# Making one pair of output-projection weights in the other order, and shifting side steps in the attention heads of a hybrid decoder layer

## The chip, the cores and the metric

The kernel runs on one core of one Trainium2 chip. The metric is the device time of one execution, in microseconds. Three runs of the kernel before gave 2347.37, 2345.92 and 2347.12 us, a median of 2347.12 us. Engines are named as the profile names them: PE multiplies matrices, DVE is the vector engine, ACT the scalar engine, POOL the GpSimd engine, SP the engine that issues most of the DMA transfers.

## The reference

One layer with 1024 tokens and 2048 features in float32: normalise, project to the queries, keys, values and gates of two groups of eight heads, run stick-breaking attention on one group and differential attention on the other, gate, project out, add to the residual, then a second gated projection of an embedding and a final norm. Cut to what matters here:

```python
hn = rmsnorm(x, norm_mix_g)
sb_q, sb_k, sb_v, sb_g, df_q, df_k, df_v, df_g = split(hn @ w_in)
sb_out = stick_breaking_attention(sb_q, sb_k, sb_v)        # 8 heads of 128
df_out = differential_attention(rope(df_q), rope(df_k), df_v, lam)   # 8 heads, 2 x 64 query/key columns
mixed = concat([sb_out * silu(sb_g), rmsnorm(df_out) * silu(df_g)])
h = x + mixed @ w_out                                       # the output projection
h = h + sigmoid(rmsnorm(h) @ w_ple_gate) * (p @ w_ple_proj)
return rmsnorm(h) * norm_final_g
```

## The kernel before

Activations are held transposed, with 128 features on the partitions and the tokens in two halves of 512. A float32 product is three matmuls: each operand is split into a high part, rounded to the PE's fast float32 form, and a low part, the rest; high times high, high times low and low times high go into one PSUM bank. Splitting is one ACT instruction (the high part) and one DVE instruction (the low part).

The program runs in five stages, one after the other: the projection to values and gates; the heads of token half 1; the heads of token half 0; the output projection; the gate projection with the final norm. The values-and-gates projection and the output projection save multiplications with seven products in place of eight (Strassen's scheme in Winograd's form), over sums of quarter blocks; the class `Seven` holds what they share.

**The heads.** Each head is a unit of 32 triples of matmuls (lines 263 to 265) that make the head's queries and keys. After every triple the program calls `side.tick()`, which advances a counter and runs the side steps that have come due: the attention of the head before, the gates, the loading and splitting of later operands. A step's due time is a number in the tables at the head of the file, counted in triples. A due time therefore sets only the place of the step's instructions in the program. Each engine works through its own instructions in that order and stops at one whose operand is not there. PE, DVE and ACT keep the written order; for SP and POOL a scheduler in the build places the transfers.

Steps and lines that the prediction speaks of:

- `taken` of a stick-breaking head (line 1611) multiplies the finished query or key sums by the row factors on DVE; the high parts follow on ACT (line 1619), the low parts on DVE (line 1614), and then the scores can start (lines 341 to 343).
- In the differential heads of half 0 a score block z (lines 345 and 346) lies in a PSUM tile of which there are two. It is masked and reduced to a row maximum on DVE (line 326), then exponentiated on ACT (line 402), which lets the tile go. Each head has eight such blocks, two for each of four groups of query rows.
- `turn` and `mix` transpose the finished weights (line 484), split them (lines 501 to 507) and multiply by the values (lines 527 to 532). `norm` sums squares with a small matmul (line 573).
- At the seam, the last unit of half 1, `swap` loads the normalised input of half 0 over that of half 1, as `late_x0`: line 1352 issues the load, and some ticks later lines 1355 (ACT) and 1356 (DVE) split it.

**The output projection.** It has two phases of eight columns of blocks, u = 0 to 7. In the second phase PE runs, for each u, the products A11(u), A22(u-1), S2(u), S4(u-1), A12(u), S1(u), S3(u), each of twelve matmuls (lines 713 to 715). After each product `step` prepares weights for a later one: `whigh` casts the high part on ACT (line 804, or 802 for S4, which is negated), `wlow` subtracts for the low part on DVE (line 818, or 816 for S4). The weights are made in a fixed order, about four products ahead of their use, into a ring of nine tiles. The sources are four raw quarter blocks B11, B12, B21, B22 of the weight matrix and three differences made on DVE (line 769): T1 = B12 - B11 and T2 = B22 - T1 with S2, T3 = B12 - B22 with S3, T4 = B21 - T2 with A22. B21 is the source of A12, and T4 is the last reader of B21: right behind T4 the program issues the load of B21 for the next u (line 760). `u3` (line 1968, shown as u) adds the S3 sums to the A11 result on DVE; the next A22 product goes into the same PSUM bank and must wait for it. Lines 1848 to 1856 are the sums for the next stage's operands, which follow the stored rows by fixed steps.

The order in which the weights are made is the list that `flow` returns:

```python
def flow(n):
    return [(ph, u, nm) for ph in range(2) for u in range(n) for nm in (("A11", "A12") if ph else ()) + ("S2", "S1", "S3", "S4", "A22")]
```

Of the kernel before, what the change touches and what calls it, by code (L numbers as in the profile page):

```python
# [31 lines left out]
EPS = 1e-6  # L32
SUB_EPS = 1e-5

SC = ((6.5, 7, 9.0, 11.5, 15.5, 17.5, 20.0, 21.5), (10.5, 10.5, 15.5, 23.0))
TT = ((19, 31, 16.0), (21.5, 36.5, 20))
DGAP = (3, 7.0)
DF0 = (0.5, 1, 1.5, 3.5, 5.5)
DF1 = (1, 1.0, 3, 5, 6.5)
LV = ((3.0, 4.0), (1, 2))  # L40
LT = ((1, 1.5), (0.5, 2.0))
LM = ((0.5, 2.0, 4, 5), (1.5, 2.5, 4.5, 6.5))
LN = ((1, 6.0), (1, 4.5))
PRIO = 300
NORM_LAT = ((8.0, 8.5), (13, 11))
XLAT = 5
SBB = ((20, 20, 15, 15.5, 16, 16.5, 16.5, 16.0), (19.5, 8.5, 5.0, 3.5, 4.0, 5.5, 5.0, 3.0))
SBS = ((0.5, 3.5, 15.5, 23.5), (-2.5, 3, 7.0, 13.0))
SBT = ((15, 31, 13), (16.0, 30.0, 14.5))
SGAP = (3.5, 6.0)  # L50
SBL = ((1.5, 3, 6.0), (1, 2, 8.0))
SVG = ((18, 37.5, 40, 40, 46), (30.5, 37.5, 41.0, 43.5, 49.5))
CST = (16.5, 19.5)
ROPE = ((-0.4, 1.5, 3.0, 4.0, 2.2, 4.5, 6.0, 7.0), (-1.9, -1, 0, 1, 0.20000000000000018, 2, 3, 4))
ROPE_ = ((3.5, 4.0, 6.0, 10.0, 11.6, 12.5, 15.0), (6.5, 7, 9.5, 12.5, 12.6, 13.5, 14))
VGD = ((19.5, 37, 37.0, 39.5, 44.0), (22.5, 32.5, 35.5, 37.0, 45.0))
LAM0 = 0.8 - 0.6 * math.exp(0.0)
NEG = -1.0e30
EXTRA = 5, 9
PIECES = 30  # L60
LOWG = ORDER1[H - 1:H + 1]
LAST = ((2.5, 3.5), (2, 4.0))
X1T = 1, 2.5, 4, 5.5, 9, 10.5, 12, 13.5
VLAG = 3

# [6 lines left out]
def _body(ctx, nc, tc, ap):  # L72
# [174 lines left out]
    side = Side()  # L247
# [66 lines left out]
    def attention(at, pz, half, hd, q, qz, K, KL, VV, sg, vg, state):  # L314
# [45 lines left out]
        def weights(rb, c):  # L360
# [3 lines left out]
            if sb:  # L364
# [125 lines left out]
        def parts(pr, g, tp, wh, wl):  # L490
# [18 lines left out]

            side.later(1 if sb else LT[half][0], high)  # L510
            side.later(2 if sb else LT[half][1], low)

        def mix(pr, g):
# [33 lines left out]

            side.later(2 if sb else LM[half][1], summed)
            if sb:
# [15 lines left out]

            side.later(LM[half][2], squared)
            side.later(LM[half][3], low)

        def norm(pr):
# [25 lines left out]

            side.later(LAST[half][0], roots)
            side.later(LAST[half][1], step)

        n0 = nb // 2
        n1 = n0 - 1  # L600
        gap = SGAP[half]
        if sb and half == 1 and hd == ORDER1[-1]:
            b = SBB[1][hd]
            ss, t0, t1, tv = [[b], [b + 4], [b + 10], [b + 15]], b + 17, b + 30, b + 14
        elif sb:
            b = SBB[half][hd]
# [11 lines left out]
        for pr, t, n in ((0, t0, n0), (1, t1, n1)):  # L618
# [5 lines left out]
            if not sb:  # L624
                steps.append((t + gap * n + NORM_LAT[half][pr], partial(norm, pr)))
        return steps

    with tc.tile_pool(name="at", bufs=2) as at, ExitStack() as banks:
# [26 lines left out]
        def ftile():  # L655
            return ev.tile([P, HALF], F32, name="hc", tag="f", bufs=4)

        def flow(n):
            return [(ph, u, nm) for ph in range(2) for u in range(n) for nm in (("A11", "A12") if ph else ()) + ("S2", "S1", "S3", "S4", "A22")]

        class Seven:

# [580 lines left out]
        for ph in range(2):  # L1243
            for u in range(2 * H):
                last = ph == 1 and u == 2 * H - 1
# [115 lines left out]

        op = Seven(lambda u, ph, k: ap["w_out"][u, ph, k], 8, flow(8))
        tw_d = dram.tile([8, 2, P, 2, HALF], F32, name="tw_d", tag="tw_d")
        hcomb_d = dram.tile([4, 8, P, HALF], F32, name="hcomb_d", tag="hcomb_d")
        q_d = dram.tile([8, 2, P, HALF], F32, name="q_d", tag="q_d")
# [152 lines left out]
        for half in (1, 0):  # L1520
# [5 lines left out]
            for hd in (ORDER0, ORDER1)[half]:  # L1526
# [27 lines left out]
                if half == 1 and hd == ORDER1[-1]:  # L1554
                    def late_x0(kt, wait):
                        with tc.issue_after(lastw[0].ins):
                            side.add([(wait, load_x0(kt))])

                    def swap(pc):
                        for i, kt in enumerate((pc * 2, pc * 2 + 8, pc * 2 + 1, pc * 2 + 9)):  # L1560
                            if pc < 2:
                                side.add([(1 + 4 * i, load_x0(kt))])
                            else:
                                side.add([(1 + i, partial(late_x0, kt, 4 + 3 * i))])

                    side.add([(8 * pc + 7, partial(swap, pc)) for pc in range(4)])

# [35 lines left out]
                if sb:  # L1603
# [26 lines left out]
                    side.add([(28, partial(taken, 0)), (31, partial(taken, 1))])  # L1630
                    side.add([(t, fn) for t, fn in zip(SVG[half], (load_vg, partial(normed, 0), partial(normed, 1), gate, gated))])
                    if half == 0 and hd == ORDER0[-1]:
                        last_steps()
                    unit(X, acc=acc)
                    q, k, qz, KL = qk[0], qk[1], None, None
                else:
# [63 lines left out]
                    q, k, qz, KL = qk[0], qk[1], qk["qz"], qk["kl"]  # L1700
# [21 lines left out]
                if half == 1 and hd >= H or half == 0 and 1 < hd < 6:  # L1722
                    kt = KT[hd if half else hd - 2]
# [759 lines left out]
```

## Time and profile before

| what | value |
|---|---|
| median of three runs | 2347.12 us |
| the profiled execution's own time | 2344.73 us |
| its span, first to last instruction | 2342.9 us |
| PE busy | 2300.4 us (98%) |
| DVE busy | 1828.0 us (78%) |
| ACT busy | 1170.5 us (50%) |
| heads of half 1 | from 619.5 us to 1062.8 us |
| heads of half 0 | from 1062.8 us to about 1640 us |
| output projection, second phase | from 1800.8 us to about 1965 us |

The times of the last three rows are the starts of the matmuls concerned in the trace. The span is 1.8 us shorter than the time of the same execution, which holds what lies before the first and behind the last instruction. In a row of the timeline the first number is the start in microseconds from the start of the span, the second the duration, then come engine, line, operation, and the tiles as output<-inputs; a bracket at the end gives the idle time of the engine before the instruction and what ended it. Tile names are shortened: T stands for T1 to T4 alike, u for u2 and u3, wpr for a ring tile of weights.

### The profile page before, as it was taken

What the parts mean: (1) busy time and instruction counts of PE and PEld (TensorE: products, weight loads), DVE (VectorE), ACT (ScalarE), POOL (GpSimd) and SP (SyncE); (2) the same over time, 40 slices, a digit from 0 to 9 for tenths busy, and PEclk for the clock granted to TensorE, in tenths of its full rate; (3) what the DMA queues carried; (4) which work ended last, traced back from release to release, by engine and by line L of the source; (5) the groups of instructions that cost most, each with busy time, mean ns of one, the idle gap of its engine ahead of it and who ended that gap; (6) DMA issues with size and microseconds to landing.
All of it is one profiled execution on the core that took longest, in us unless ns stands there. A gap on an engine that the chain in (4) does not pass through costs nothing.

```text
span 2342.9 us, 32443 instructions
## 1 busy us (share of the span) xinstructions
PE 2300.4 (98%) x10976; PEld 1916.2 (82%) x10976; DVE 1828.0 (78%) x3181; ACT 1170.5 (50%) x2184; POOL 345.4 (15%) x486
## 2 busy tenths in 40 slices
PE   9999999999999999999999999999999999999997
PEld 7888888888888878887888888888888877888886
DVE  7699786777678877777888876668887887788788
ACT  6334243333267776445677765445633335533544
POOL 1211112223200030000001101101111232000000
PEclk9999999999999999999999999999999999999998
DMA  7699579999977788787756666678888778898666
GB/s 254 225 307 354 175 240 288 293 279 265 310 252 252 256 269 314 262 259 245 223 176 189 194 202 208 201 215 244 211 220 217 227 227 278 277 336 290 239 230 218
DMA packets 266549, 581.01 MB, mean 248 GB/s; under 512 B 30032, under 2 KB 58960, under 8 KB 266384
## 3 DMA queue, kind: packets, MB, share of 16 engines
q1 hardware_dynamic: 191776, 394.35, 49.8%
q0 software_dynamic: 55312, 149.71, 24.4%
q10 hardware_dynamic: 19296, 34.90, 4.3%
q8 instruction: 86, 1.41, 0.2%
q14 instruction: 79, 0.65, 0.1%
HBM read 373.32 MB, written 213.91 MB: 251 GB/s over the span
## 4 chain that ended last, share of the span: by engine, by line
PE 76%; DMA 10%; DVE 8%; ACT 4%; issue 1%; SPq 0%; ACTq 0%; DVEq 0%
PE acc L265 8%; PE acc L263 8%; PE acc L264 8%; PE pbc L713 6%; PE pbc L715 6%; PE pbc L714 6%; DMA wlo<-wlo_d 3%; PE pa L714 2%; PE pa L713 2%; PE pa L715 2%; PE tp L484 2%; DMA wraw<-w_gate 2%; DMA wraw<-w_out 2%; PE pb L715 1%; PE pb L713 1%
## 5 line engine op out<-in xcount | busy, mean ns | idle before, releaser
L804 ACT CAST wpr<-T 128x512 fp32r<-128x512 f32 x208 | 125.1, 621 | 484.2 <-DVE T L769 391.6
L263 PE MATMUL acc<-xh,whi 128*128 128x512 f32 x768 | 312.5, 407 | 0.0
L265 PE MATMUL acc<-xh,wlo 128*128 128x512 f32 x768 | 302.0, 393 | 4.7 <-DMA wlo<-wlo_d 4.7
L264 PE MATMUL acc<-xl,whi 128*128 128x512 f32 x768 | 300.9, 392 | 0.0
L265 PEld LDWEIGHTS acc<-xh,wlo 128*128 128x128 f32 x768 | 144.6, 188 | 40.3 <-DMA wlo<-wlo_d 8.5
L264 PEld LDWEIGHTS acc<-xl,whi 128*128 128x128 f32 x768 | 145.4, 189 | 23.7
L263 PEld LDWEIGHTS acc<-xh,whi 128*128 128x128 f32 x768 | 144.9, 189 | 23.6 <-DVE qk L1611 0.3
L804 ACT CAST wpr<-wraw 128x512 fp32r<-128x512 f32 x144 | 88.3, 617 | 140.5 <-DMA wraw<-tw_d 31.3
L818 DVE TENSOR_TENSOR wpr<-T,wpr 128x512 fp32r<-128x512 f32 x208 | 142.5, 685 | 4.7 <-ACT wpr L804 2.1
L946 POOL DMA_DIRECT2D vg_d<-hc x120 | 88.6, 770 | 287.9 <-DVE hc L943 128.9
L502 ACT CAST awh<-tp 128x256 fp32r<-128x256 f32 (+1 forms) x160 | 80.5, 503 | 80.4 <-PE tp L484 74.8
L507 DVE TENSOR_TENSOR awl<-tp,awh 128x256 fp32r<-128x256 f32 (+1 forms) x160 | 92.4, 577 | 35.1 <-ACT awh L502 34.6
L713 PE MATMUL pbc<-cS,wpr 128*128 128x512 f32 x288 | 112.0, 389 | 0.0
L714 PE MATMUL pbc<-cS,wpr 128*128 128x512 f32 x288 | 112.0, 389 | 0.0
L715 PE MATMUL pbc<-cS,wpr 128*128 128x512 f32 x288 | 112.0, 389 | 0.0
L326 DVE CUSTOM_DVE_ANT_0 z<-z,masks 128x512 f32<-128x512 f32 (+7 forms) x128 | 96.9, 767 | 19.0 <-PE z L346 9.8
L818 DVE TENSOR_TENSOR wpr<-wraw,wpr 128x512 fp32r<-128x512 f32 x144 | 97.2, 682 | 11.3 <-ACT wpr L804 11.3
L378 DVE TENSOR_TENSOR_SCAN st<-pt 128x511 f32<-128x511 f32 (+3 forms) x64 | 86.7, 1354 | 23.5 <-ACT pt L371 22.5
L371 ACT ACTIVATE pt<-z 128x512 f32<-128x512 f32 (+3 forms) x64 | 41.7, 652 | 77.3 <-DVE z L354 75.4
L532 PE MATMUL av<-awl,v 128*128 128x256 f32 x256 | 73.0, 285 | 1.2 <-DVE awl L507 1.2
L530 PE MATMUL av<-awh,v 128*128 128x256 f32 x256 | 72.0, 281 | 0.7 <-ACT awh L502 0.7
L531 PE MATMUL av<-awh,v 128*128 128x256 f32 x256 | 72.4, 283 | 0.0
(596 smaller groups left out, 6833.7 us busy)
## 6 DMA issues: line engine op xcount, KB each, us to landing
wlo<-wlo_d SPq DMA_DIRECT2D x94, 512.0 KB, 5.2
whi<-whi_d SPq DMA_DIRECT2D x74, 512.0 KB, 4.1
wraw<-w_vg SPq DMA_DIRECT2D x129, 256.0 KB, 4.2
vg_d<-hc POOLq DMA_DIRECT2D x120, 256.0 KB, 5.5
wraw<-w_in SPq DMA_DIRECT2D x54, 512.0 KB, 5.0
wraw<-w_gate SPq DMA_DIRECT2D x92, 256.0 KB, 5.1
wraw<-w_out SPq DMA_DIRECT2D x72, 256.0 KB, 4.6
wlo_d<-wlo SPq DMA_DIRECT2D x34, 512.0 KB, 3.4
```

What stands on the lines that cost most here:

```text
L263: T.matmul(acc[c], hi[:, k2, kh, c, :], xh, start=first, stop=False)
L264: T.matmul(acc[c], hi[:, k2, kh, c, :], xl, start=False, stop=False)
L265: T.matmul(acc[c], lo[:, k2, kh, c, :], xh, start=False, stop=last)
L326: V.tensor_tensor_reduce(z, z, mwide[:, 0:n], -DF_SCALE, 3.0e38, ALU.add, ALU.min, mx)
L378: V.tensor_tensor_scan(st[:, off + 1:nkey], pt[:, off:nkey - 1], pt[:, off:nkey - 1], initial=1.0, op0=ALU.mult, op1=ALU.bypass)
L507: V.tensor_tensor(wl[:, o, :], tp[:, o, :], wh[:, o, :].bitcast(F32), op=ALU.subtract)
L713: T.matmul(o, wh[:, w], xh, start=start and k == 0, stop=False, skip_group_check=True)
L714: T.matmul(o, wh[:, w], xl, start=False, stop=False, skip_group_check=True)
L715: T.matmul(o, wl[:, w], xh, start=False, stop=k == 3, skip_group_check=True)
L804: A.copy(t[:, 0], src)
L818: V.tensor_tensor(t[:, 1], src, t[:, 0].bitcast(F32), op=ALU.subtract)
L946: G.dma_start(vg_d[hf, blk, u], o, **(dict(accum_op=ALU.add) if ph else {}))
```

## The change

Three things are changed. No operation is added or removed, and what is computed stays the same.

1. The output projection makes its weights in the order S2, S1, S3, A22, S4; the values-and-gates projection keeps S2, S1, S3, S4, A22.
2. At the seam, the splits of the eight blocks of half 0 that are loaded last come two ticks later behind their loads.
3. Due times in the tables are shifted by half a tick to three ticks: in half 0 the first score blocks (SC), values (TT), splits of turned weights (LT), squares (LM), the first norm (NORM_LAT), rotation (ROPE), gates (VGD, SVG) and, for the stick-breaking heads, the distance between groups of turned weights (SGAP) and two score times; in half 1 the stick-breaking heads' last score block (SBS), their sigmoids (SBL) and gates (SVG). The first numbers of a pair in a table are those of half 0, the second those of half 1.

```diff
-SC = ((6.5, 7, 9.0, 11.5, 15.5, 17.5, 20.0, 21.5), (10.5, 10.5, 15.5, 23.0))
-TT = ((19, 31, 16.0), (21.5, 36.5, 20))
+SC = ((7.0, 8.5, 9.0, 11.5, 15.5, 17.5, 21.0, 21.5), (10.5, 10.5, 15.5, 23.0))
+TT = ((19, 31, 17.0), (21.5, 36.5, 20))
...
-LT = ((1, 1.5), (0.5, 2.0))
-LM = ((0.5, 2.0, 4, 5), (1.5, 2.5, 4.5, 6.5))
+LT = ((1, 2.0), (0.5, 2.0))
+LM = ((0.5, 2.0, 4, 6.0), (1.5, 2.5, 4.5, 6.5))
...
-NORM_LAT = ((8.0, 8.5), (13, 11))
+NORM_LAT = ((11.0, 8.5), (13, 11))
...
-SBS = ((0.5, 3.5, 15.5, 23.5), (-2.5, 3, 7.0, 13.0))
+SBS = ((0.5, 3.5, 15.5, 23.0), (-2.5, 3, 7.0, 11.0))
...
-SGAP = (3.5, 6.0)
-SBL = ((1.5, 3, 6.0), (1, 2, 8.0))
+SGAP = (4.0, 6.0)
+SBL = ((1.5, 3, 6.0), (1.5, 2, 8.0))
...
-LAST = ((2.5, 3.5), (2, 4.0))
+LAST = ((2.0, 3.0), (2, 4.0))
...
-        def flow(n):
-            return [(ph, u, nm) for ph in range(2) for u in range(n) for nm in (("A11", "A12") if ph else ()) + ("S2", "S1", "S3", "S4", "A22")]
+        def flow(n, last=("S4", "A22")):
+            return [(ph, u, nm) for ph in range(2) for u in range(n) for nm in (("A11", "A12") if ph else ()) + ("S2", "S1", "S3") + last]
...
-        op = Seven(lambda u, ph, k: ap["w_out"][u, ph, k], 8, flow(8))
+        op = Seven(lambda u, ph, k: ap["w_out"][u, ph, k], 8, flow(8, ("A22", "S4")))
...
-                                side.add([(1 + i, partial(late_x0, kt, 4 + 3 * i))])
+                                side.add([(1 + i, partial(late_x0, kt, (6 if pc == 2 else 6) + 3 * i))])
```

Three places show what the new numbers do to the order of instructions.

DVE in the second phase of the output projection, one u, first before. The rows run from the last sum of one u (line 1983) over T3 = T_17989 and T4 (the second line 769, written over T2 = T_17935) to the A22 and S4 results of lines 1869:

```order
L1983 TENSOR_TENSOR s_17809<-s_17809,hr 128x512
L769 TENSOR_TENSOR T_17989<-wraw,b_16470 128x512
L818 TENSOR_TENSOR wpr<-T_17932,wpr 128x512
L818 TENSOR_TENSOR wpr<-T_17989,wpr 128x512
L1869 TENSOR_TENSOR hc<-pbc,s_17809 128x512
L769 TENSOR_TENSOR T_17935<-wraw,T_17935 128x512
L816 SCALAR_TENSOR_TENSOR wpr<-b_16470,wpr 128x512
L1946 TENSOR_TENSOR u_18041<-pbc,s_17975 128x512
```

and the same place with the change:

```order
L1983 TENSOR_TENSOR s_17809<-s_17809,hr 128x512
L769 TENSOR_TENSOR T_17989<-wraw,b_16457 128x512
L818 TENSOR_TENSOR wpr<-T_17932,wpr 128x512
L769 TENSOR_TENSOR T_17935<-wraw,T_17935 128x512
L818 TENSOR_TENSOR wpr<-T_17989,wpr 128x512
L1869 TENSOR_TENSOR hc<-pbc,s_17809 128x512
L818 TENSOR_TENSOR wpr<-T_17935,wpr 128x512
L1946 TENSOR_TENSOR u_18040<-pbc,s_17975 128x512
```

T4 moves ahead of two instructions: the low part of the S3 weights and the A22 result, which reads a finished PE product. The low part of S4 moves behind line 1946.

DVE at the seam; acc_9645 is the sum of the last head's keys, and xl_9889 (xl_9890 with the change) the first of the eight late blocks:

```order
 L507 TENSOR_TENSOR awl<-tp,awh 128x512
-L1356 SCALAR_TENSOR_TENSOR xl_9889<-xl_9889,gvec,xh_9888 128x512
 L1614 TENSOR_TENSOR q<-qk,q 128x512
 L1611 TENSOR_TENSOR qk<-acc_9645,ssa 128x512
+L1356 SCALAR_TENSOR_TENSOR xl_9890<-xl_9890,gvec,xh_9889 128x512
 L1614 TENSOR_TENSOR k<-qk,k 128x512
```

The late block's low part moves behind the low part of the queries and behind the multiplication of the key sums. On ACT the order at this place does not change: the late block's high part (line 1355) stays ahead of the high part of the keys (line 1619).

PE in a differential head of half 0, at the first score blocks:

```order
-L345 MATMUL z<-k,q 128x512
-L346 MATMUL z<-kl,qz 128x512
-L345 MATMUL z<-k_10608,q 128x512
-L346 MATMUL z<-kl,qz 128x512
 L263 MATMUL acc_10615<-xh_9719,whi 128x512
 L264 MATMUL acc_10615<-xl_9720,whi 128x512
 L265 MATMUL acc_10615<-xh_9719,wlo 128x512
-L573 MATMUL msq<-sqh,onesr 128x256
-L574 MATMUL msq<-sql,onesr 128x256
 L345 MATMUL z<-k,q 128x512
 L346 MATMUL z<-kl,qz 128x512
```

The first block moves one triple back, to the place of the second; the second moves back too, to one triple ahead of the third, which stays where it was. The two norm matmuls move three triples back, behind the third block.

More of the change, by code (lines that the diff above doesn't have):

```diff
@@ L39 @@
 DF1 = (1, 1.0, 3, 5, 6.5)
-LV = ((3.0, 4.0), (1, 2))
-LT = ((1, 1.5), (0.5, 2.0))
-LM = ((0.5, 2.0, 4, 5), (1.5, 2.5, 4.5, 6.5))
-LN = ((1, 6.0), (1, 4.5))
+LV = ((1.0, 5.5), (1, 2))
+LT = ((1, 2.0), (0.5, 2.0))
+LM = ((0.5, 2.0, 4, 6.0), (1.5, 2.5, 4.5, 6.5))
+LN = ((1, 3.0), (1, 4.5))
 PRIO = 300
-NORM_LAT = ((8.0, 8.5), (13, 11))
+NORM_LAT = ((11.0, 8.5), (13, 11))
 XLAT = 5
-SBB = ((20, 20, 15, 15.5, 16, 16.5, 16.5, 16.0), (19.5, 8.5, 5.0, 3.5, 4.0, 5.5, 5.0, 3.0))
-SBS = ((0.5, 3.5, 15.5, 23.5), (-2.5, 3, 7.0, 13.0))
+SBB = ((20, 20, 16.5, 15.5, 16, 16.5, 16.5, 16.0), (19.5, 8.5, 5.0, 3.5, 4.0, 5.5, 5.0, 3.0))
+SBS = ((0.5, 3.5, 15.5, 23.0), (-2.5, 3, 7.0, 11.0))
 SBT = ((15, 31, 13), (16.0, 30.0, 14.5))
-SGAP = (3.5, 6.0)
-SBL = ((1.5, 3, 6.0), (1, 2, 8.0))
-SVG = ((18, 37.5, 40, 40, 46), (30.5, 37.5, 41.0, 43.5, 49.5))
-CST = (16.5, 19.5)
-ROPE = ((-0.4, 1.5, 3.0, 4.0, 2.2, 4.5, 6.0, 7.0), (-1.9, -1, 0, 1, 0.20000000000000018, 2, 3, 4))
+SGAP = (4.0, 6.0)
+SBL = ((1.5, 3, 6.0), (1.5, 2, 8.0))
+SVG = ((18, 37.5, 40, 40, 45.5), (30.5, 37.5, 40.0, 42.5, 48.5))
+CST = (17.5, 19.5)
+ROPE = ((-1.9, 1.5, 3.0, 4.0, 2.2, 4.5, 6.0, 7.0), (-1.9, -1, 0, 1, 0.20000000000000018, 2, 3, 4))
 ROPE_ = ((3.5, 4.0, 6.0, 10.0, 11.6, 12.5, 15.0), (6.5, 7, 9.5, 12.5, 12.6, 13.5, 14))
-VGD = ((19.5, 37, 37.0, 39.5, 44.0), (22.5, 32.5, 35.5, 37.0, 45.0))
+VGD = ((19.5, 37.5, 37.5, 40.0, 44.5), (22.5, 32.5, 35.5, 37.0, 45.0))
 LAM0 = 0.8 - 0.6 * math.exp(0.0)
```

## The prediction, on record before the run

> **What bounds the kernel now.** I read the page first, then the waits, then the stretches of the second phase of the output projection, and last the timeline where PE stands still.
>
> ```profile
> span 2342.9 us, 32443 instructions
> PE 2300.4 (98%) x10976; PEld 1916.2 (82%) x10976; DVE 1828.0 (78%) x3181; ACT 1170.5 (50%) x2184; POOL 345.4 (15%) x486
> ```
>
> PE is busy but for 42.6 us of the span, and the change takes no matmul away. It can win only in those 42.6 us and where PE runs slowly. The waits of PE, longest sums first, show where:
>
> ```profile
> PE pbc L713 <- DVE u L1968: 5.2, 5, 1.9
> PE acc L265 <- DMA wlo<-wlo_d: 4.7, 8, 1.1
> PE z L341 <- ACT k L1619: 2.2, 1, 2.2
> PE acc L263 <- DVE qk L1611: 1.6, 1, 1.6
> ```
>
> Columns are the sum in us, the number and the longest. The first row is the second phase of the output projection, the third the seam between the halves. Two short stretches show what else a long wait costs (PE's clock is the third number from the end):
>
> ```profile
> 1070.20:1073.60 3.40, 3.40 (x10) 2.64 (x9) 3.22 (x8) 2.06 (x4) 0.31 (x1) 0.51 0.93 260
> 1903.10:1906.50 3.40, 3.40 (x9) 2.62 (x10) 3.33 (x5) 0.35 (x1) 1.76 (x1) 0.50 0.48 186
> ```
>
> Right behind the wait of 2.24 us at the seam and that of 1.88 us in the output projection, PE runs 3.4 us at half clock, which loses 1.7 us each time. The waits of 1.6 us and less have no such stretch behind them.
>
> **The weight order: a loop that is longer than PE's work.** The second phase by its u, from one A11 product to the next:
>
> ```profile
> 1838.85:1857.89 19.04, 19.04 (x86) 15.77 (x85) 14.54 (x22) 6.75 (x13) 6.13 (x7) 1.00 0.74 217
> 1857.89:1877.42 19.53, 19.33 (x86) 15.69 (x84) 15.47 (x23) 7.27 (x13) 7.12 (x8) 1.00 0.81 241
> 1877.42:1898.19 20.77, 19.34 (x86) 15.69 (x85) 16.22 (x25) 7.27 (x13) 6.81 (x8) 1.00 0.77 226
> 1898.19:1921.02 22.83, 20.95 (x86) 16.82 (x84) 18.11 (x26) 7.26 (x13) 7.35 (x9) 0.93 0.71 210
> 1921.02:1940.75 19.73, 19.34 (x85) 15.70 (x84) 15.84 (x24) 7.27 (x13) 7.05 (x8) 1.00 0.79 226
> 1940.75:1961.68 20.93, 19.54 (x85) 15.53 (x84) 20.67 (x31) 10.44 (x18) 7.76 (x9) 1.00 0.90 290
> ```
>
> Seven products are 84 matmuls, 19.04 us undisturbed (0.227 us each). The five later stretches are 0.49, 1.73, 3.79, 0.69 and 1.89 us over that: 8.6 us, half clock included. Why the sums are late is told by ACT, DVE and PE, one u:
>
> ```profile
> 1886.48 0.68 DVE L769 TENSOR_TENSOR T<-wraw 128x512 f32<-128x512 f32 x1
> 1887.09 1.46 DVE L818 TENSOR_TENSOR wpr<-T,wpr 128x512 fp32r<-128x512 f32 x2
> 1888.46 0.68 DVE L1869 TENSOR_TENSOR hc<-pbc,s 128x512 f32<-128x512 f32 x1
> 1889.07 0.68 DVE L769 TENSOR_TENSOR T<-wraw,T 128x512 f32<-128x512 f32 x1
> 1895.96 0.62 ACT L804 CAST wpr<-wraw 128x512 fp32r<-128x512 f32 x1 [4.52 <-DMA wraw<-w_out]
> 1897.77 1.27 DVE L1848 SCALAR_TENSOR_TENSOR hq<-hc,gvec,hq 128x512 f32<-128x512 f32 x1 [4.29 <-ACT hq L1847]
> 1902.21 0.69 DVE L1968 TENSOR_TENSOR u<-pbc,s 128x512 f32<-128x512 f32 x1
> 1902.95 0.69 PE L713 MATMUL pbc<-cA,wpr 128*128 128x512 f32 x1 [1.88 <-DVE u L1968]
> ```
>
> T4 (1889.07) frees B21; its reload reaches ACT's cast for A12 at 1895.96, 6.89 us later. ACT and, behind it, DVE stand idle for it. DVE starts again at 1897.77 and comes to the sum that PE needs 4.44 us later, without a pause. The cycle closes through the same work one u earlier:
>
> ```profile
> 1880.99 0.68 DVE L1968 TENSOR_TENSOR u<-pbc,s 128x512 f32<-128x512 f32 x1
> 1839.05 0.69 DVE L1968 TENSOR_TENSOR u<-pbc,s 128x512 f32<-128x512 f32 x1 [0.17 <-PE pbc L715]
> ```
>
> From that sum to T3 DVE needs 5.49 us (1880.99 to 1886.48), from T3 to T4 2.59. So the loop takes 6.89 + 1.81 + 4.44 + 5.49 + 2.59 = 21.2 us against PE's 19.04, and loses 2.2 us per u once the slack is gone.
>
> With the change T4 stands right behind T3 and one low part: 1886.48 + 2 x 0.61 = 1887.70, 1.37 us earlier. The S3 low part and the A22 result move behind T4 and each come 0.6 us later. Behind them nobody waits: S3's product is five products away, and the A22 result only goes to memory. The S4 low part, and with it the reload of B22, comes some 2 us later, for weights used eight products on. The loop becomes 19.85 us, 0.8 us per u over PE's work. At 1839.05 the sum waited for PE itself, so the slack there is whole, 1.8 us (it ends at 1839.74; A22 follows the A11 product, at 1838.85 + 2.73 = 1841.58). Earlier T4s keep it whole one u longer. Then 0.8 us a u uses it up in about two u's, and the last two or three A22 products wait 0.5 to 0.8 us each, too short for half clock. So 1.6 us of the 8.6 stay: **-7.0 us**. Bounds: 0, if the load lands no earlier, and -8.6.
>
> **Start of the projection.** The A22 weights also take S4's place once at its start:
>
> ```profile
> 1697.37 0.69 DVE L695 TENSOR_TENSOR cS<-cS 128x512 fp32r<-128x512 f32 x1 [0.61 <-ACT cS L689]
> 1697.78 0.56 ACT L1736 COPY hc<-pa 128x512 f32<-128x512 f32 x1
> 1698.39 0.50 PE L713 MATMUL pb<-cS,wpr 128*128 128x512 f32 x1 [0.22 <-ACT hc L1736]
> 1705.17 0.50 PE L713 MATMUL pbc<-cS2h,wpr 128*128 128x512 f32 x1 [0.71 <-ACT wpr L804]
> ```
>
> The copy at 1697.78 frees the bank that PE waits for. Ahead of it stood the cast of S4, ready at once; now stands that of A22, which waits for T4, and T4 stands behind line 695: T4 at 1697.98, cast at 1698.7, copy at 1699.2, PE at 1699.85 in place of 1698.39. Two products later PE waits 0.71 us for other weights, which come as before, so half of the 1.45 us vanishes: **+0.5 us**, bounds 0 and +3.2 (all of it, and half clock).
>
> **The seam.**
>
> ```profile
> 1057.66 2.86 SPq L1352 DMA_DIRECT2D xl<-h_d  x4
> 1065.60 0.72 ACT L1355 ACTIVATE xh<-xl,gvec 128x512 fp32r<-128x512 f32 x1 [3.62 <-DMA xl<-h_d]
> 1066.35 0.75 DVE L1356 SCALAR_TENSOR_TENSOR xl<-xl,gvec,xh 128x512 fp32r<-128x512 f32 x1 [3.50 <-ACT xh L1355]
> 1067.62 0.68 DVE L1611 TENSOR_TENSOR qk<-acc,ssa 128x512 f32<-128x512 f32 x1
> 1068.34 0.62 ACT L1619 CAST k<-qk 128x512 fp32r<-128x512 f32 x1 [2.02 <-DVE qk L1611]
> 1069.01 0.49 PE L341 MATMUL z<-k,q 128*128 128x512 f32 x1 [2.24 <-ACT k L1619]
> 1069.74 0.50 PE L342 MATMUL z<-k,q 128*128 128x512 f32 x1 [0.23 <-DVE k L1614]
> ```
>
> ACT waits 3.62 us for the first late block. DVE stands at that block's low part just as long, and behind it queue the query low part and the key multiplication; then ACT's key cast; then PE. Two ticks later the block's low part stands behind the key multiplication. DVE does both in the wait. ACT still has the late block ahead of the key cast, so the cast comes right behind it, at 1066.1 in place of 1068.34, and ends at 1066.75; PE was ready at 1066.77. The key low part follows the late block's: 1067.0 to 1067.7, so PE pauses about 0.5 us before line 342. Of 2.47 us of waiting 0.5 stay, and there is no half clock: 2.0 + 1.7 = **-3.7 us**. Bounds: 0, if the load lands 2 us later, and -4.4 with what a restart costs.
>
> **The shifted steps in the heads.** PE issues the same matmuls; its few waits there can move.
>
> ```profile
> 1211.81 0.40 PE L345 MATMUL z<-k,q 128*128 128x512 f32 x1
> 1212.94 1.23 DVE L326 CUSTOM_DVE_ANT_0 z<-z,masks 128x1024 f32<-128x1024 f32 x1
> 1214.27 1.12 ACT L402 ACTIVATE et<-z,mx 128x1024 f32<-128x1024 f32 x1
> 1216.66 0.34 PE L345 MATMUL z<-k,q 128*128 128x384 f32 x1
> 1058.92 0.51 PE L527 MATMUL av<-lead,v 128*128 128x256 f32 x2 [0.98 <-DVE lead L506]
> ```
>
> The first score block's tile is let go at 1215.39 and taken by the third at 1216.66: 1.27 us to spare. The first block moves one triple (0.68 us) back and the norm pair (0.24 us) from between them to behind: 0.35 us to spare, no wait. The wait of 0.98 us near the seam loses the late low part ahead of line 506: -0.4. For the other shifts (gates half a tick, wider spacing of turned weights in half 0) I see only waits under 0.8 us that can close, and the eight waits for wlo, 4.7 us together, whose loads keep their place. I take **-0.8** for these, bounds -4 (the wlo waits gone) and +4 (doubled).
>
> Sum: -7.0 + 0.5 - 3.7 - 0.4 - 0.8 = -11.4 us. The profiled execution, 2344.7 us, would become 2333.3; it lies 2.4 us under the median of the runs, so I expect 2347.1 - 11.4 = **2335.7 us**.
>
> [...]
>
> **Rivals.** *The load is not earlier.* B21's reload then lands when it did, since it now follows B12's reload on SP by about 1.2 us instead of 2.6, and DMA carries 211 to 226 GB/s there. The first term falls to about -1: 2341.7. Against it: 256 KB need little over a microsecond at that rate. Chance 0.12.
>
> *The half clock stays.* If it is not these gaps that halve the clock, 3.4 us come back: 2339.1. Only the place of the two stretches, right behind the two longest gaps, speaks against it; chance 0.05.
>
> *The seam's stall stays*, because the load of the late block, not the order, holds ACT, and the key cast is behind it in both orders: 2339.4. For it: 8 us from issue to use. Chance 0.08.
>
> *Waits for score tiles, slower than before.* If mask and exponential of the first block come later than I reckon, because DVE or ACT is still at older work, PE waits in all eight differential heads of half 0. Price: eight times the lateness beyond 0.35 us. From 1.8 us late the whole gain is eaten; at waits of 1.9 us each adds 1.7 us of half clock, 8 x 3.6 = 29 us, and the time is 2364. the row of line 326 shows no wait of DVE before it, so DVE may be the later one; its 1.27 us to spare speak against it. Chance 0.09.
>
> *Small losses*: the many shifted steps cost about what they win and the wlo waits double: 2343 to 2347. Chance 0.08.
>
> **How the numbers follow.** The forecast keeps 0.58; its own range is 2331 to 2339. The range reaches to the first three rivals and part of the last: 2330.5 to 2345.0; about 0.2 is left out. A measurement of this kernel can tell about 0.2%, 4.7 us. Faster by more: forecast, half clock, seam and half of the first rival, 0.76; within: 0.15; slower: 0.09.
>
> **What would show it.** Right: in the second phase T4 directly behind T3 and one low part, ACT's A12 cast 1.3 us or more earlier behind T4's place, stretches of 19.0 to 19.9 us, no half clock at 1903; at the seam a PE wait under 0.8 us and no half clock; a wait of 1 to 1.6 us at the first S1 product. Wrong: stretches over 20 us; a wait of 2 us at line 341; waits of PE for line 402 in the differential heads.

## The result, and the profile after

The changed kernel takes 2332.10 us, the median of six runs (2329.97 to 2336.93), against 2346.78 us for six runs of the kernel before. The ratio is 0.9940 with a 95% interval from 0.9929 to 0.9952: 14.7 us faster by the medians, 11.3 to 16.7 us by the interval. The forecast was 11.4 us faster, 2335.7 us, and the result lies in its own range of 2331 to 2339 us.

The profiled execution took 2333.76 us, 1.7 us over its median, while that of before lay 2.1 us under the median of the six runs. The two traces therefore differ by only 11.0 us. Its page begins:

```profile
span 2331.8 us, 32460 instructions
PE 2297.7 (99%) x10976; PEld 1916.5 (82%) x10976; DVE 1821.7 (78%) x3181; ACT 1168.8 (50%) x2184; POOL 342.0 (15%) x486
```

PE stands still for 34.1 us where it was 42.5, and its busy time is 2.7 us shorter for the same matmuls. Half clock is not the reason, since this profile too has two stretches of it, in other places (behind waits for wlo at 1203 and 1421 us). In the trace of the change the first 128x512 matmul behind a wait takes 0.47 to 0.50 us, where one in the stream takes 0.39 us and starts 0.227 us behind the last, and there are fewer waits now; that this makes up the 2.7 us is not shown. The waits of PE that lead now or that the prediction spoke of, with the sum, the number and the longest:

```profile
PE acc L265 <- DMA wlo<-wlo_d: 5.6, 5, 1.7
PE z L341 <- ACT k L1619: 0.8, 1, 0.8
PE pb L713 <- ACT hc L1736: 0.8, 1, 0.8
PE av L527 <- DVE lead L506: 0.5, 1, 0.5
PE pbc L713 <- ACT wpr L804: 0.4, 1, 0.4
```

The first row of before, line 713 behind line 1968, is gone from the list. The waits for wlo now lead it. The second phase of the output projection, one stretch per u (length, then PE, PEld, DVE, ACT and POOL busy with their counts, PE's clock, DMA's share and rate):

```profile
1838.97:1858.01 19.04, 19.04 (x85) 15.77 (x84) 16.10 (x24) 7.07 (x13) 6.46 (x8) 1.00 0.81 238
1858.01:1877.05 19.04, 19.04 (x85) 15.77 (x84) 16.37 (x24) 7.14 (x14) 6.57 (x8) 1.00 0.82 249
1877.05:1896.09 19.04, 19.04 (x85) 15.77 (x84) 16.45 (x24) 7.24 (x14) 6.70 (x9) 1.00 0.85 250
1896.09:1915.13 19.04, 19.04 (x85) 15.77 (x84) 16.12 (x24) 7.15 (x13) 6.48 (x8) 1.00 0.83 249
1915.13:1934.17 19.04, 19.04 (x85) 15.77 (x84) 16.29 (x24) 7.17 (x13) 6.69 (x9) 1.00 0.80 232
```

Every stretch is 19.04 us, PE's own work, at full clock. DVE now reaches the sum on line 1968 early and waits for PE, as the timeline of that place shows:

```profile
1877.25 0.69 DVE L1968 TENSOR_TENSOR u<-pbc,s 128x512 f32<-128x512 f32 x1 [1.21 <-PE pbc L715]
1882.38 0.69 DVE L769 TENSOR_TENSOR T<-wraw 128x512 f32<-128x512 f32 x1
1883.58 0.69 DVE L769 TENSOR_TENSOR T<-wraw,T 128x512 f32<-128x512 f32 x1
1888.42 0.62 ACT L804 CAST wpr<-wraw 128x512 fp32r<-128x512 f32 x1 [1.62 <-DMA wraw<-w_out]
1896.29 0.69 DVE L1968 TENSOR_TENSOR u<-pbc,s 128x512 f32<-128x512 f32 x1 [1.48 <-PE pbc L715]
```

T3 is at 1882.38, T4 1.20 us behind it, and ACT's cast for A12 4.84 us behind T4, where before it took 6.89. At the seam:

```profile
1065.04 0.72 ACT L1355 ACTIVATE xh<-xl,gvec 128x512 fp32r<-128x512 f32 x1 [4.70 <-DMA xl<-h_d]
1065.66 0.60 ACT L1619 CAST k<-qk 128x512 fp32r<-128x512 f32 x1
1066.32 0.50 PE L341 MATMUL z<-k,q 128*128 128x512 f32 x1 [0.84 <-ACT k L1619]
1067.20 0.50 PE L342 MATMUL z<-k,q 128*128 128x512 f32 x1 [0.38 <-DVE k L1614]
```

ACT still stands for the late block, and the key cast follows it at once. PE waits 1.22 us there in place of 2.47 and keeps its clock.

Stage by stage, from the starts of PE's matmuls in the two traces: half 1 up to the start of half 0 is 1.6 us shorter, the first unit of half 0 a further 1.7 us, the rest of the heads of half 0 3.7 us longer, the first phase of the output projection 0.3 us shorter, the second phase 8.7 us, and the gate projection with the final norm 2.5 us. In a second profile of the change, from the last experiment below, the rest of the heads of half 0 is 0.2 us shorter than before and the gate projection 0.6 us. These two parts hang on loads that land at other times in each execution, as the next section shows.

### The profile page after: what moved, and what is told of

Read it like the earlier page. It is cut to its first block, busy times and chain, and to the rows that moved or that the text cites. A ratio compares the mean times of both kernels' runs of the same rounds, so it can differ in the third digit from the quotient of the medians.

```text
span 2331.8 us, 32460 instructions
## 1 busy us (share of the span) xinstructions
PE 2297.7 (99%) x10976; PEld 1916.5 (82%) x10976; DVE 1821.7 (78%) x3181; ACT 1168.8 (50%) x2184; POOL 342.0 (15%) x486
## 4 chain that ended last, share of the span: by engine, by line
PE 86%; DMA 5%; DVE 5%; ACT 2%; issue 1%; SPq 0%; DVEq 0%; POOL 0%; ACTq 0%
PE acc L265 9%; PE acc L263 9%; PE acc L264 8%; PE pbc L713 7%; PE pbc L715 7%; PE pbc L714 7%; PE pa L715 3%; PE pa L713 3%; PE pa L714 3%; DMA wlo<-wlo_d 3%; PE tp L484 2%; PE pb L2002 2%; PE pb L2001 2%; PE pb L2000 2%; PE pb L714 1%; PE pb L713 1%
```

## The experiments

Each kernel's ratio is against runs of the kernel before on the same chip, with its 95% interval. 0.001 is 2.35 us.

**The three parts alone.** Each takes the kernel before and one part of the change: the order of the weights,

```diff
+        op = Seven(lambda u, ph, k: ap["w_out"][u, ph, k], 8, flow(8, ("A22", "S4")))
```

the late splits,

```diff
+                                side.add([(1 + i, partial(late_x0, kt, 6 + 3 * i))])
```

and all due times of the tables (the diff of the change without these two; besides the tables named above it moves the half-0 numbers of LV, LN, CST and LAST).

> The kernel before with only the new weight order in the output projection. Theory A (the loop T4, reload of B21, sums, next T3 was longer than PE's work): all stretches of the second phase come to 19.0 us, PE's five waits at line 713 for line 1968 and the half clock go, the second phase is 8 to 8.6 us shorter, and the whole kernel 7 to 10 us faster than before. The reload of B21 takes 4 to 4.5 us and not 5.5 to 6.2. Theory B (the second phase became shorter because the shifted steps ahead of it left SP's and POOL's queues in another state): the stretches stay over 20 us and the kernel is within 3 us of before.

> The kernel before with only the splits of the late blocks two ticks later. Theory A: PE's wait of 2.24 us at line 341 falls to 0.5 to 0.9 us, the wait at line 342 is 0.2 to 0.5 us, no half clock follows, and the stretch from the last unit of half 1 to the first of half 0 and on to the second is 2.5 to 3.5 us shorter; the whole is 2 to 4 us faster. Theory B (the load holds ACT whatever the order on DVE): the wait stays over 2 us and the time is that of before. Theory C (half clock has another cause than the wait): the wait falls but PE still runs 3.4 us at half clock near 1070 us, and 1.2 us are won.

> The kernel before with only the shifted due times. The traces of before and after differ in the heads by -0.4 us in half 1, about -0.8 us at the lead wait, and +3.7 us in half 0, where waits for wlo grow. Theory A (as predicted: the shifts are worth little): between 3 us faster and 3 us slower than before. Theory B (the shifts carry the 3 us by which the whole change did better than forecast): 3 to 6 us faster. Theory C (the longer waits for wlo in half 0 come from the shifts and stay): 2 to 4 us slower.

The weight order alone gave 0.9981 (0.9972 to 0.9990), the late splits alone 0.9979 (0.9970 to 0.9988), the due times alone 0.9986 (0.9976 to 0.9997): 4.5, 4.9 and 3.3 us. Their sum, 12.7 us, agrees with the whole change within the intervals. (By the medians it is 5.9, 5.9 and 3.9 us, the numbers that a later expectation uses.) The weight order thus won less than the 7 to 10 us of its theory A.

With the weight order alone all waits of 0.3 us or more at line 713 for line 1968 go from the second phase, as theory A had it, but two other waits come, one at each end of the projection:

```profile
PE z L341 <- ACT k L1619: 2.5, 1, 2.5
PE pbc L713 <- DVE hq L1974: 2.0, 1, 2.0
PE pb L713 <- ACT hc L1736: 1.6, 1, 1.6
```

The last is the copy behind the A22 cast at the first S1 product, 1.64 us, where the prediction had reckoned 1.45 us more than the 0.22 of before. The second is at the last u: DVE stands 2.52 us for ACT's split of a gate operand, which waits for its load, and line 1974 is queued behind it; half clock follows. In the whole change that wait is 0.27 us in one profile and 0.87 us in the other. From the first A11 product to the first matmul of the gate projection the second phase takes 161.6 us here, 167.0 us before and 158.3 us with the change, so 5.4 us were won in it; the start of the projection takes 0.9 us of them away.

With the late splits alone the waits at lines 341 and 342 are

```profile
1067.54 0.50 PE L341 MATMUL z<-k,q 128*128 128x512 f32 x1 [0.61 <-ACT k L1619]
1068.42 0.50 PE L342 MATMUL z<-k,q 128*128 128x512 f32 x1 [0.38 <-DVE k L1614]
```

without half clock, and that unit is 2.9 us shorter: theory A, with a time that won somewhat more than its 2 to 4 us (2.8 to 7.0). With the due times alone the same place gets worse, because half 0 starts 1.1 us earlier against a load that does not land earlier:

```profile
1069.24 0.79 PE L341 MATMUL z<-k,q 128*128 128x512 f32 x1 [3.06 <-ACT k L1619]
```

Even so the due times won 3.3 us (0.7 to 5.6), so neither theory A at its centre nor C holds. What they close can be read from the traces: the lead wait near the seam (0.98 us before, 0.5 us at its new place), 0.9 us at the first scores of a differential head, 0.3 us at one wait for the query sums in half 1, and 0.8 us of waits for turned weights in half 0 (lines 530 and 532: 1.9 us before, 1.1 us with the change).

**Both halves of the due times.** The changed kernel with all due times of before, and with those of half 0 alone put back:

> The changed kernel with all due times of before: new weight order and late splits alone. Alone these two won 5.9 and 5.9 us, the shifted due times 3.9 us. Theory A (the parts add up): 10 to 12 us faster than before, 3 to 4 us less than the whole change. Theory B (the due times won only because they moved the seam, or are worth nothing beside the other parts): 13 to 15 us faster than before, as the whole change. Theory C (the shifts are worth more once the seam is free, since without it the half 0 starts earlier into the same load): 8 to 10 us faster than before.

> The changed kernel with the due times of half 0 as before: new weight order, late splits and the shifts of half 1 alone. The traces give half 1 0.4 us, mostly at one wait for the query sums, and 0.8 us at the lead wait near the seam; in half 0 the wait of 0.9 us at the first scores of a differential head and some 1 us of waits for turned weights go. Theory A (both halves carry it): 12 to 13 us faster than before, 1 to 1.5 us more than without any shift. Theory B (half 0 carries all): as without any shift. Theory C (the shifts of half 0 cost, by waits for wlo): 14 to 17 us faster, more than the whole change.

Without the shifts the ratio was 0.9958 (0.9944 to 0.9971), 9.9 us; with those of half 1 alone 0.9944 (0.9928 to 0.9959), 13.1 us. The first lies between theories A (10 to 12 us) and C (8 to 10 us), and its interval, 6.8 to 13.1 us, holds both; what it speaks against is that the shifts are worth nothing beside the other parts. The second lies where both halves carry a part, but its interval reaches to either of its rivals, so how the shifts' worth divides between the halves stays open.

**Why B21's reload is shorter.** It took 5.5 to 6.2 us in the last five u's before and 4.0 to 4.5 us with the change. Over all profiles the two ranges overlap: 4.6 to 7.0 us, median 5.65, in five kernels with the old order, and 3.6 to 6.4 us, median 4.45, in eight with the new one and the reload right behind T4. Rows of the view of the transfers, in one window of before and one of after, show the case (size, median time to landing):

```profile
h_d<-hc POOLq DMA_DIRECT2D x1, 256.0 KB, 6.1
wraw<-w_out SPq DMA_DIRECT2D x1, 256.0 KB, 6.1
```

```profile
wraw<-w_out SPq DMA_DIRECT2D x1, 256.0 KB, 4.0
```

Before, B22's reload was issued 0.6 us behind it and a store on POOL's queue 0.4 us ahead of it. With the change B22's comes 3.7 us later, and both stores of POOL there come just behind. One run keeps the old order and lets only B22's reload wait:

```diff
-                if then:
+                if then and self.st and key[2] == "S4":
+                    self.hold.append((self.late + 3, then))
+                elif then:
                     then()
+                if self.hold and self.hold[0][0] <= self.late:
+                    with tc.issue_after(self.st[-1].ins):
+                        self.hold.pop(0)[1]()
```

> The kernel before with the old weight order, but the reload of B22 is issued behind the stores of the sums, some 4 us later than B21's reload instead of 0.6 us. It asks why B21's reload took 4.0 to 4.5 us with the change and 5.5 to 6.2 us before. Theory A (the two reloads share the DMA engines): B21's reload takes 4 to 4.5 us, the loop falls from 21.2 to about 19.6 us, the second phase loses 2 to 3 us instead of 8.6, and the whole is 5 to 7 us faster. Theory B (it is the stores on POOL's queue, issued just ahead of B21's reload before and just behind it with the change): B21's reload stays at 5.5 us or more, and the time is within 2 us of before.

The ratio is 0.9995 (0.9984 to 1.0005), and B21's reload takes 5.1 to 6.8 us over the same five u's. B22's reload is not the cause. That it is POOL's stores was left as the other theory and not tried at this place, so it is not shown. In the run below that makes the reload wait, it stands 0.7 us behind such a store again and takes 4.2 to 5.5 us, between the two cases; the cause stays open.

**Is it the loop?** The next run was to delay B21's reload in the changed kernel:

```diff
-                    self.wload(n + 1, 21)
+                    if len(self.units) != 16:
+                        self.wload(n + 1, 21)
...
+ partial(self.wload, n + 1, 21) if nm == "A22" and len(self.units) == 16 else None))
```

> The changed kernel, but the reload of B21 is issued behind the low part of A22 and not right behind T4: 1.8 us later, with T4 in its new place. In the runs so far the time from one u3 to the next is the sum of its parts to within 0.1 us: u3 to T3, T3 to T4, 0.75 us to the issue, the load's own time, 6.25 us from ACT's A12 cast to the next u3. Theory A (that loop is what was cured): it becomes 5.5 + 1.2 + 1.8 + 0.75 + 5.5 to 6 + 6.3 = 21 to 21.5 us, the waits at line 713 for line 1968 come back in the last four or five u's, and the kernel loses 6 to 10 us of its 14.7. Theory B (T4's place on DVE matters, the load's does not): no waits come back, time as with the change.

It gave 0.9941 (0.9925 to 0.9957) and tells nothing of the theories: SP's scheduler put the reload 0.75 us behind T4 all the same, since nothing made it wait. It stands as a repetition of the change. In its profile B21's reload took 3.7 to 6.4 us, and the slack took up what the two longest cost: no wait at the line that is 1968 before. The following run makes it wait, by a DVE instruction that reads B21 later:

```diff
+            def late21(self, n):
+                if n >= 8:
+                    V.tensor_tensor(self.t4[:, 0:P], self.B[21][:, 0:P], self.t4[:, 0:P], op=ALU.subtract)
+                self.wload(n + 1, 21)
```

> What the run before was meant to do: there the build's scheduler put the reload of B21 right behind T4 again, so that it was the changed kernel once more. Here a small instruction of DVE (0.2 to 0.3 us, once per u in the second phase) reads B21 behind the low part of A22, so the reload must wait for it: some 2 us later, T4 in its new place. Theory A (the loop is what was cured): from one u3 to the next 5.5 + 1.2 + 0.75 + 2 + 5 to 6 + 6.3 = 20.8 to 21.8 us where nothing is idle; waits at line 713 for line 1968 come back in the last four u's, and the kernel loses 5 to 9 us of its 14.7. Theory B (the place of T4 on DVE matters, the load's does not): no waits, time as with the change but for some 2 us of DVE's work that nobody waits for.

The ratio is 0.9985 (0.9976 to 0.9995): 11 of the 14 us are lost, more than the 5 to 9 expected. The second phase takes 165.9 us, 7.6 of these 11; the rest has no place in the loop and lies within the noise of the two ratios. The waits are back (line 1975 is line 1968 of this kernel), and the timeline shows the longer loop:

```profile
PE pbc L713 <- DVE u L1975: 6.1, 5, 2.1
```

```profile
1887.64 0.69 DVE L774 TENSOR_TENSOR T<-wraw,T 128x512 f32<-128x512 f32 x1
1890.16 0.29 DVE L753 TENSOR_TENSOR T<-wraw,T 128x128 f32<-128x128 f32 x1
1895.42 0.62 ACT L811 CAST wpr<-wraw 128x512 fp32r<-128x512 f32 x1 [4.56 <-DMA wraw<-w_out]
1901.68 0.68 DVE L1975 TENSOR_TENSOR u<-pbc,s 128x512 f32<-128x512 f32 x1
```

T4 keeps its new place here, so it is the loop that was cured, not T4's place on DVE. In u's where no part of the loop waits for PE, the parts add up, as in these three:

| kernel | u3 to T3 | T3 to T4 | T4 to issue | load | cast to u3 | sum | measured |
|---|---|---|---|---|---|---|---|
| before | 5.49 | 2.58 | 0.74 | 6.08 | 6.25 | 21.14 | 21.22 |
| order alone | 5.49 | 1.21 | 0.75 | 5.45 | 6.26 | 19.16 | 19.23 |
| change, reload made to wait | 5.48 | 1.20 | 2.88 | 4.83 | 6.26 | 20.65 | 20.73 |

The rest of 0.08 us is from landing to cast. PE needs 19.04 us. In the change's profile no such u occurs in the second half of the phase: the loop without its idle time is 17.6 to 17.8 us. In the profile of its repetition two occur, with reloads of 5.34 and 6.41 us and loops of 19.3 and 20.3 us, each between u's that win back slack.

**Later splits, and the start of the projection.** The changed kernel with the late splits two more ticks later, and with the new weight order only in the second phase:

```diff
-                                side.add([(1 + i, partial(late_x0, kt, (6 if pc == 2 else 6) + 3 * i))])
+                                side.add([(1 + i, partial(late_x0, kt, 8 + 3 * i))])
...
-("S2", "S1", "S3") + last]
+("S2", "S1", "S3") + (last if ph else ("S4", "A22"))]
```

> The changed kernel with two more steps. The late blocks' splits come four ticks later than before, so that ACT's key cast stands ahead of the first late block: Theory A: PE's waits at lines 341 and 342, 0.84 and 0.38 us with the change, vanish. And the weights have the new order only in the second phase of the output projection: the wait at the first S1 product falls from 0.81 to about 0.2 us, that two products on rises to about 0.7. Together 1 to 1.5 us faster than the change: 0.9935 of before. Theory B: the late splits now hold up the score work behind them, PE waits elsewhere at the seam for as long, and the time is that of the change.

0.9948 (0.9932 to 0.9965), no better than the change. The waits at lines 341 and 342 do vanish, but the late splits now come later on DVE, and the lead wait behind them grows from 0.5 us:

```profile
1087.79 0.48 PE L527 MATMUL av<-lead,v 128*128 128x256 f32 x2 [2.41 <-DVE lead L506]
```

That is theory B. At the start of the projection 0.75 us of waiting stays in place of 0.81 and 0.40, too little to see in the time.

**The waits that now lead.** PE's waits for wlo in half 0 come at the start of a unit. Among the transfers issued within 4 us at one such place of the change are

```profile
comb_d<-sg POOLq DMA_DIRECT2D x3, 256.0 KB, 8.3
k<-k_d POOLq DMA_DIRECT2D x1, 512.0 KB, 4.9
whi<-whi_d SPq DMA_DIRECT2D x1, 512.0 KB, 7.7
wlo<-wlo_d SPq DMA_DIRECT2D x1, 512.0 KB, 9.8
comb_d<-sg SPq DMA_DIRECT2D x1, 256.0 KB, 2.3
```

Three accumulating stores of the finished head, issued by POOL, stand ahead of the unit's first weights, which land late. One run makes two of the three stores wait until the middle of the unit:

```diff
-        G.dma_start(S2, t, accum_op=ALU.add)
-        G.dma_start(S4, t, accum_op=ALU.add)
+        def rest():
+            if hd not in (5, 6, 7):
+                V.tensor_tensor(t[:, 0:2], t[:, 0:2], t[:, 0:2], op=ALU.max)
+            G.dma_start(S2, t, accum_op=ALU.add)
+            G.dma_start(S4, t, accum_op=ALU.add)
+
+        if hd in (5, 6, 7):
+            rest()
+        else:
+            side.later(13, rest)
```

> The changed kernel, and in half 0 two of the three accumulating stores of a finished head come 13 ticks later (behind a DVE instruction of 0.1 us that rewrites two columns of the tile with themselves). With the change the three stores and a key load are issued within 2 us ahead of the unit's first whi and wlo, which take 8 to 10 us to land in place of 4 to 5, and PE waits for wlo in five of the units, 5.6 us together, with two short stretches at half clock. Theory A (these stores hold the loads up): the loads at the start of a unit land in 5 to 7 us, the waits for wlo in half 0 fall to under 2 us, and it is 4 to 6 us faster than the change, 0.992 of before. Theory B (the stores only move: loads later in the unit wait): time of the change, with waits at other blocks of wlo.

The ratio is 0.9923 (0.9909 to 0.9936), 18 us faster than before. The same place now reads

```profile
whi<-whi_d SPq DMA_DIRECT2D x1, 512.0 KB, 6.7
wlo<-wlo_d SPq DMA_DIRECT2D x1, 512.0 KB, 7.3
comb_d<-sg SPq DMA_DIRECT2D x1, 256.0 KB, 2.2
comb_d<-sg POOLq DMA_DIRECT2D x1, 256.0 KB, 5.4
```

and a stretch of 100 us of the heads of half 0, first of the change, then of this kernel, shows PE's gain (length, then PE busy):

```profile
1200.00:1300.00 100.00, 96.15 (x505) 81.11 (x504) 81.83 (x171) 73.26 (x141) 9.23 (x13) 0.98 0.58 176
```

```profile
1200.00:1300.00 100.00, 100.00 (x538) 85.28 (x537) 87.16 (x187) 77.32 (x151) 10.98 (x15) 1.00 0.64 190
```

No wait for wlo of 0.3 us or more is left in half 0 but one of 0.37 us at its start. To see what this has to do with the change, the last two runs put the later stores alone on the kernel before, and the change beside it on the same chip:

> The kernel before, and only the two accumulating stores of each finished head of half 0 come 13 ticks later. With the change this ended all waits for wlo in half 0. Theory A (those waits have nothing to do with the change): the eight waits of the kernel before, 4.7 us together, end here too, and it is 4 to 6 us faster than before, 0.998 of it; the rest (seam, second phase) stays as it was. Theory B (it is the shifted steps of the change that made room): some of the waits stay, 0 to 2 us faster.

> The changed kernel once more, beside the same runs of the kernel before as the kernel with only the later stores, to set its time beside that with the later stores added (0.9923 of before). Theory A (the later stores beat the change): 0.993 to 0.995 of before, with four to six waits for wlo of 0.5 to 1.9 us in half 0 and no wait at line 713 for line 1968. Theory B (the difference was of another chip): 0.992 to 0.993.

The later stores alone give 0.9977 (0.9968 to 0.9986), 5.4 us, and one wait for wlo of 0.32 us is left: they work without the change. In that kernel a wait of 0.32 us for turned weights shows in each of six differential heads; it stays away where the due times are shifted. The change again gives 0.9940 (0.9926 to 0.9954). The later stores on top of it are thus the fastest version here, by 0.0017 or 4 us; the intervals of the two overlap a little, and the two were not run side by side.

## Why the prediction was right

**The weight order** was forecast at -7.0 us with a bound of -8.6. The second phase is 8.7 us shorter by the two traces, but the trace of before was the longest of its kind there: it holds a stretch at half clock, which only two of the five profiles with the old order have. These five take 165.5 to 167.0 us for the phase, 166.1 in the mean, and seven with the new order and the late splits together 158.2 to 159.3 us, 158.8 in the mean, so the order is worth 7.3 us in this phase. The mechanism is the one named, as the run with the reload made to wait shows; that the forecast came so near is in part luck, for two errors cancel. One is the 8.6 us, which took half clock for a part of every execution. The other is the step "1.6 us of the 8.6 stay". It took the load's time over from before: a loop of 19.85 us held 6.89 us from T4 to the cast. With the reload issued earlier the load itself took 4.0 to 4.5 us, which leaves 4.84 us from T4 to the cast, and the loop fell below PE's work. With the order alone, where three loads still took 5.3 to 5.5 us, the loop was 19.2 us in two u's and lost 0.2 us in each. So the rival that the load would land no earlier did not come; the load took less time too.

**The start of the projection**, +0.5 us, was right in kind: 1.64 us of waiting at the first S1 product with the order alone, where 1.67 had been reckoned, and the wait two products on gone. With the shifted due times it is 0.81 and 0.40 us, 0.3 us over before. The shifts' part in this had not been foreseen.

**The seam**, -3.7 us: the order of events was right, and the half clock went with the wait. The wait was forecast at 0.5 us and is 1.0 us with the late splits alone and 1.2 us in the change. The mis-sized term is the moment at which the late block lands: the key cast came 0.6 us after the block in all cases, but against the moment when PE was ready the block landed 0.5 and 0.7 us later than in the profile of before. The 1.7 us of half clock are again the price of one execution: with the old seam and a wait of 2.2 us or more at line 341, four of five profiles have it. Two ticks more on the late splits only move the wait to the lead product.

**The lead wait and the other shifts**, -1.2 us together: probably too small. They gave 3.3 us alone (0.7 to 5.6), and the change loses 4.2 us without them; both are uncertain by more than 2 us, and the first holds the forecast. The waits that the traces show closing come to 2.3 us. The step "I see only waits under 0.8 us that can close" failed: a wait of 0.9 us for a differential head's first scores fell to 0.2 us, and the sentence did not add up the many short ones in both halves. That the score tiles of the differential heads would be late, the slower rival, did not come: there is one wait of 0.32 us for line 402, in the first of them.

**The half clock.** The rival that it stays was wrong for the two stretches named. But the change's own profile has two new ones, behind waits of 1.38 and 1.67 us for wlo, so the sentence that waits of 1.6 us and less have none behind them holds for the profile of before and not for the change. Here a wait's length alone did not tell whether half clock followed it, as the counts in the last section show. The granted clock of the timed runs, 0.9964 in the mean of 33 of before and 0.9972 of six of the change, makes the net gain about 2 us (an estimate, the difference times the span) in place of the 3.4 us that were counted.

The sum, 11.4 us, lies just inside the interval of the result, 11.3 to 16.7 us, so that it was short at all is not clear of the noise. Term by term the weight order came 0.3 us over its forecast, the shifts 1.1 us, and the seam's waits 0.7 us under theirs. The gate projection's 2.5 us in the traces are no part of it: its two waits for the split of loaded values, 0.64 and 0.84 us before, were none in the change, but one of 1.43 us in the run that was to delay the reload.

## What to carry to other kernels

When a row of stretches is longer than the bounding engine's own work and the engine in front of it waits for a load, close the loop once around and write it as a sum; the sum tells what an instruction's place is worth before it is moved. A load's time is part of what a reordering changes: here it fell from 5.65 to 4.45 us in the median, for a reason that stays open. One trace's wait and what follows it is one execution's, so take a price from several profiles where they are at hand. And the scheduler here undid a later place in the program where nothing made the transfer wait (it put the reload 0.75 us behind T4 all the same), so look at the order before believing an experiment, or at its trace.

## What the runs showed of the hardware

In all 14 profiles the 13 stretches at half clock between 20 and 2300 us begin at whole multiples of 3.413 us after the clock first rose to full, and each lasts 3.413 us (one of them twice that). If each trace is cut into pieces of that length from that moment on, all 12 pieces in which PE stood still for more than 1.8 us in sum were followed by half clock, one of 15 with 1.6 to 1.8 us, and none of 40 with 1.2 to 1.6 us. With less there is one of over 9000: the first half of the stretch that lasted twice as long, in the kernel with the due times alone, and why it went on is open. In these profiles, then, half clock goes with how long PE stood still within such a piece, 1.67 us or more of 3.413 but for that one, and not with the length of one wait alone. Pieces of the trace, of the change and of the kernel with later splits (length, then PE busy; PE's clock is the third number from the end; the last row is the stretch right behind the wait):

```profile
1199.71:1203.12 3.41, 1.59 (x8) 0.87 (x7) 3.35 (x9) 3.14 (x7) 0.00 (x0) 1.00 1.02 373
1203.12:1206.53 3.41, 3.41 (x12) 2.83 (x11) 1.54 (x3) 0.84 (x3) 0.00 (x0) 0.50 0.06 25
```

```profile
1083.57:1086.99 3.42, 1.81 (x8) 1.16 (x7) 2.48 (x7) 1.49 (x5) 0.55 (x1) 1.00 0.75 271
1086.99:1090.40 3.41, 2.61 (x16) 2.38 (x17) 1.79 (x5) 1.28 (x2) 0.00 (x0) 1.00 0.96 290
1087.80:1091.20 3.40, 3.40 (x19) 2.99 (x20) 1.78 (x6) 1.87 (x2) 0.00 (x0) 1.00 0.97 326
```

In the first, waits of 0.44 and 1.38 us fall into one piece, 1.82 us in sum, and PE runs the next at half clock. In the second a longer wait, of 2.41 us, is cut by the border into 1.60 and 0.80 us, and the clock stays full. Counted by the wait alone (granted clock under 0.95 in the 3.6 us behind it), half clock followed 1 of 52 waits of PE of 1.2 to 1.6 us, 5 of 22 of 1.6 to 2.0 us and 7 of 12 over 2.0 us. Where a wait would fall among the pieces was not known before the run. So for this kernel a wait near 2 us should be priced with a third to a half of the 1.7 us that such a stretch loses (an estimate from these counts, 12 of the 34 waits over 1.6 us), not with all or nothing, and short waits that lie close together should be added up.

In the change's profile loads of 512 KB (whi and wlo) landed in 4.9 us in the median of the heads of half 0. Where POOL had issued two or three accumulating stores of 256 KB within 2.5 us ahead of them, those of whi took 6.7 to 9.5 us and those of wlo 7.4 to 11.2 us. With two of the three stores moved away the longest load took 8.2 us, though POOL still issues a load of keys at the same place.
